# A two-layer decoder trunk in split fp32: a fourth Strassen block in the second MLP product, and the gate weights in the ring of activations

## The chip, the cores and the metric

One Trainium2 chip, one NeuronCore of it. The metric is the device time of one execution in microseconds; the figure for the kernel before is the median of three executions. Five engines appear in the profile: PE (TensorE, matrix products), DVE (VectorE), ACT (ScalarE), POOL (GpSimd) and SP (which only issues transfers here). Each engine works through its own list of instructions in a fixed order and waits on semaphores of the others.

## The reference, cut to what matters

Two layers, 256 tokens, width 2048. Layer 0 mixes by a gated convolution and differential attention, layer 1 by forgetting attention; after each comes a dense MLP with hidden width 8192:

```python
def _sqrelu_mlp(h, w1, w2):
    return jnp.square(jax.nn.relu(h @ w1)) @ w2
...
for l in range(DEPTH):
    ...                                   # mixer of the layer, added to x
    h = _rmsnorm(x, norm2_g[l])
    x = x + _sqrelu_mlp(h, mlp_w1[l], mlp_w2[l])
```

Layer 1's mixer also has a forget gate: 16 columns of `fox_w_in`, one per head, go through a log-sigmoid and a cumulative sum and become a bias on the logits.

## The kernel before

**Split products.** Every fp32 operand of a large product is split into a high part in the fp32r format (`wh`, a copy on ACT) and the rest (`wl`, a subtraction on DVE: `split_w`, L131). A product is then three matmuls: high by high, high by low, low by high (`products`, L619, the lines L620 to L622). A weight block of 4 x 512 columns is one DMA of 1 MB into a ring `wraw` of 3, and one `wh` and one `wl` out of rings of 3 (`wspl`).

**The MLP.** `mlp` (L685) takes the hidden width in four groups `g` of 2048. For each group `hidden` (L591) makes 16 column tiles of 128 of the squared ReLU, in eight pairs of tiles, by `gemm_t` (L531, matmuls L550 and L554). Then `gemm_pair` (L624) is called twice, for output columns 0 to 1023 (n = 0) and 1024 to 2047 (n = 2). I call one such call a *pair*: four groups, two calls, two layers make 16 pairs. A pair runs over eight blocks of weights, each 256 rows by 1024 columns, and the text `KINDS` (L560) says how each block is multiplied:

- `C`, classical: 2 row tiles x 4 output quarters x 3 matmuls = 24 matmuls of 512 columns, on one split of the raw block (DVE: one `wl` of 128x2048).
- `S`, Strassen's method in Winograd's form: 7 products x 3 = 21 matmuls. DVE first builds four sums of weight tiles `T` (L637, L639, L640), and then two splits follow, of three raw tiles (`wl` 128x1536) and of `T` (`wl` 128x2048, shown as `wl<-qk`).

All eight blocks add into eight PSUM banks, which is all there are: P2, Q3, Q4 and X out of the pool `acc` (4 banks), P1, Q5, P7 and P6 out of the pool `tp` (4 banks). P1, Q5, P7 and P6 get no more products after the last `S` block. So after the matmuls of the block that follows it (`if i == KINDS.rindex("S") + 1`, L664) they are combined into a tile `E`, and `E` is added into the residual `xr`: a copy on ACT (L666) and L667, L668, L669 and two L674 on DVE. I call these the *E chain*. The other four banks end with the eighth block; four L680 on DVE add them into `xr` (`final`). These are appended to `late` and emitted by the `flush` of the next product, which takes the four `acc` banks over from them: the next pair, or the next group's `gemm_t`, or layer 1's first projection (L165 to L167).

**What sets the order.** The lines are written in the order above, but a scheduler of the framework places the instructions of each engine when the program is built, by priority and its own estimates; the built order is then fixed. `order` listings in this document show that built order.

**Gate weights.** `gw` (the 16 gate columns) and `gws` (their split) have places of their own in the pool `const`; the load is in `setup` (L247), the split in `forget_gates` (L414, L418 and L419).

Of the kernel before, what the change touches and what calls it, by code (L numbers as in the profile page):

```python
# [8 lines left out]
F32 = mybir.dt.float32  # L9
F32R = mybir.dt.float32r  # L10
AF = mybir.ActivationFunctionType
ALU = mybir.AluOpType
# [14 lines left out]
def trunk_kernel(  # L27
# [199 lines left out]
    nlam = const.tile([P, 1], F32, name="nlam")  # L227
    bfb = const.tile([P, 16], F32, name="bfb")
    GP = 16 * 32 + 96
    gw = const.tile([P, KT, 16], F32, name="gw")  # L230
    gws = const.tile([P, GP], F32R, name="gws")

    def setup():
        rows = work.tile([P, 2 * P], F32, name="y")[:, :P]
# [9 lines left out]
        for i, v in enumerate((hyb_lq1, hyb_lk1, hyb_lq2, hyb_lk2)):  # L244
            nc.scalar.dma_start(lv[:, i, :], v.broadcast_to([P, 64]))
        nc.scalar.dma_start(bfb, fox_b_f.broadcast_to([P, 16]))
        nc.scalar.dma_start(gw, fox_w_in[0, :, 3 * D:3 * D + 16].rearrange("(k p) n -> p k n", p=P))  # L247


        nc.gpsimd.memset(mask, 0.0)  # L250
# [162 lines left out]

    def forget_gates(nm):  # L414

        wv = gws[:, :KT * 32].rearrange("p (k n) -> p k n", n=32)
        nc.scalar.copy(gws[:, KT * 32:], ones[:, :96])
        nc.scalar.copy(wv[:, :, 0:16], gw)  # L418
# [138 lines left out]

    KINDS = "SCSCSCCC"  # L560

    class PairS:

# [27 lines left out]
    def hidden(nm, w, c0):  # L591

        pairs, half = [], None
        for i, kind in enumerate(KINDS):
            acc = gemm_t(nm.acts, w, c0 + 2 * i * P)
            if kind == "S":
                p = PairS()
            elif half is not None:
                p, half = PairC(half), None
            elif "C" in KINDS[i + 1:]:  # L600
                t = actp.tile([P, 4, 2, 2 * P], F32R, name="act")
                p, half = PairC(t[:, :2]), t[:, 2:]
            else:
                p = PairC(qkv.tile([P, 2, 2, 2 * P], F32R, name="v"))
            pairs.append(p)

            def take(acc=acc, p=p):
                f = qkv.tile([P, 4, CW], F32, name="qk")[:, :2].rearrange("p a (f n) -> p (a f) n", n=P)
                for j in range(2):
                    fj = f[:, 2 * j:2 * j + 2].rearrange("p t n -> p (t n)")  # L610
                    nc.scalar.copy(fj, acc[j][:, 2 * P:])  # L611
                    nc.vector.tensor_tensor(fj, acc[j][:, :2 * P], fj, ALU.add)
                f4 = f[:, :4].rearrange("p t n -> p (t n)")
                nc.vector.scalar_tensor_tensor(f4, f4, 0.0, f4, ALU.max, ALU.mult)
                p.fill(f)
            late.append(take)
        return pairs
# [6 lines left out]
    def gemm_pair(pairs, w, r0, n, r2, done):  # L624

        B = {}
        live = set()
        for i, (kind, p) in enumerate(zip(KINDS, pairs)):
            raw = wraw.tile([P, 4, CW], F32, name="raw")
            nc.sync.dma_start(  # L630
                raw.rearrange("p (k h) n -> p k (h n)", k=2),
                w[r0 + 2 * i * P:r0 + 2 * (i + 1) * P, n * CW:(n + 2) * CW].rearrange("(k p) n -> p k n", p=P))

            more = KINDS[i + 1:]
            if kind == "S":
                T = qkv.tile([P, 4, CW], F32, name="qk")
                nc.vector.tensor_tensor(  # L637
                    T[:, 0:2], raw[:, 1:3], raw[:, 0:1].broadcast_to([P, 2, CW]), ALU.add)
                nc.vector.tensor_tensor(T[:, 2], T[:, 1], raw[:, 1], ALU.add)  # L639
                nc.vector.tensor_tensor(T[:, 3], T[:, 2], raw[:, 3], ALU.add)  # L640
                wa, wb = split_w(raw[:, 1:4]), split_w(T)
            else:
                wa = split_w(raw)
            if i == 0:
# [10 lines left out]
            if kind == "S":  # L655
                for bank, f, ws, j in (
                        ("P1", 0, wa, 0), ("P2", 2, wa, 2), ("Q3", 7, wa, 1),
                        ("Q5", 5, wb, 0), ("P7", 4, wb, 1), ("P6", 6, wb, 2), ("Q4", 3, wb, 3)):
                    mul(bank, p.part(f), ws, j, "S" not in more and bank in ("P1", "Q5", "P7", "P6"))
            else:  # L660
                for k in range(2):
                    for bank, t, h in (("P2", 0, 1), ("Q3", 0, 0), ("X", 1, 0), ("Q4", 1, 1)):
# [118 lines left out]
```

## Time and profile before

| | us |
|---|---|
| median of three executions | 2185.5 (2184.15 to 2185.83) |
| the profiled execution | 2182.76 |
| its span, first to last instruction | 2181.0 |
| PE busy | 2168.9 |
| DVE busy | 1546.9 |
| ACT busy | 1053.6 |
| granted TensorE clock, mean | 1.000 |

The profiled execution lies 2.7 us under the median. The end of a matmul is modelled in the profile and reaches past the start of the next, so how fast PE goes is read from the distance between starts, not from the duration of one.

### The profile page before, as it was taken

The numbers are of one execution on the slowest core, as the hardware profiler recorded it, in microseconds if no ns is written. First come the engines' busy times: TensorE is split into PE (matmuls) and PEld (weight loads), VectorE is DVE, ScalarE is ACT, GpSimd is POOL, SyncE is SP. The second block draws the span as 40 slices with busy tenths as digits, with TensorE's granted clock in tenths as the row PEclk, the third lists the DMA queues.
The fourth block names the chain that finished last, engine by engine and source line by source line (L and its number), as shares of the span: only waits on it lengthen the run. The fifth ranks groups of instructions, "written<-read, shape, count | busy, mean of one in ns | idle before, by whom it ended". The sixth has DMA issues, their size and how long they took to land.

```text
span 2181.0 us, 26007 instructions
## 1 busy us (share of the span) xinstructions
PE 2168.9 (99%) x10724; PEld 1822.0 (84%) x10724; DVE 1546.9 (71%) x1572; ACT 1053.6 (48%) x1099; POOL 18.8 (1%) x17
## 2 busy tenths in 40 slices
PE   8999999999999999999999999999999999999999
PEld 6887888888888888888888888888888888888887
DVE  5576555779768768867856565566787697687687
ACT  6465443545445444445554454445444444444453
POOL 0000000000000000000000000000000000000000
PEclk9999999999999999999999999999999999999999
DMA  7554555555765765665655555555556656656654
GB/s 258 174 173 155 178 189 193 176 172 197 221 186 173 227 191 179 214 189 183 209 168 190 188 182 173 180 174 180 166 205 217 191 174 217 191 187 210 186 193 152
DMA packets 245241, 412.08 MB, mean 189 GB/s; under 512 B 9367, under 2 KB 144770, under 8 KB 245122
## 3 DMA queue, kind: packets, MB, share of 16 engines
q1 hardware_dynamic: 237264, 405.84, 57.6%
q10 hardware_dynamic: 7858, 4.58, 0.7%
q8 instruction: 84, 1.38, 0.2%
q14 instruction: 35, 0.29, 0.0%
HBM read 408.28 MB, written 2.11 MB: 188 GB/s over the span
## 4 chain that ended last, share of the span: by engine, by line
PE 99%; DMA 0%; DVE 0%; ACT 0%; issue 0%; SPq 0%; ACTq 0%; DVEq 0%
PE acc L550 22%; PE acc L554 11%; PE acc L165 11%; PE acc L167 11%; PE acc L166 11%; PE acc L621 8%; PE acc L622 8%; PE acc L620 8%; PE tp L622 2%; PE tp L620 2%; PE tp L621 2%; PE tp L186 1%; PE tp L307 0%; PE tp L319 0%; PE tp L495 0%; DMA ob<-in_hyb_lk_dram 0%
## 5 line engine op out<-in xcount | busy, mean ns | idle before, releaser
L139 DVE TENSOR_TENSOR wl<-raw,wh 128x2048 fp32r<-128x2048 f32 (+2 forms) x388 | 853.6, 2202 | 485.9 <-ACT wh L138 485.3
L138 ACT CAST wh<-raw 128x2048 fp32r<-128x2048 f32 (+2 forms) x388 | 712.8, 1839 | 595.4 <-PE acc L167 219.2
L550 PE MATMUL acc<-act,wh 128*128 128x512 f32 x2048 | 559.6, 395 | 0.0
L165 PE MATMUL acc<-wh,act 128*128 128x512 f32 x1024 | 413.0, 404 | 1.7 <-ACT wh L138 1.7
L166 PE MATMUL acc<-wl,act 128*128 128x512 f32 x1024 | 401.3, 392 | 2.3 <-DVE wl L139 2.3
L167 PE MATMUL acc<-wh,act 128*128 128x512 f32 x1024 | 401.4, 392 | 0.0
L550 PEld LDWEIGHTS acc<-act,wh 128*128 128x128 f32 x2048 | 350.4, 189 | 47.9 <-DVE act L128 0.6
L554 PEld LDWEIGHTS acc<-act,wl 128*128 128x128 f32 x2048 | 314.2, 189 | 43.4
L554 PE MATMUL acc<-act,wl 128*128 128x256 f32 x2048 | 325.8, 281 | 0.0
L621 PE MATMUL acc<-wl,act 128*128 128x512 f32 x656 | 255.9, 390 | 0.0
L622 PE MATMUL acc<-wh,act 128*128 128x512 f32 x656 | 255.4, 389 | 0.0
L620 PE MATMUL acc<-wh,act 128*128 128x512 f32 x656 | 251.4, 389 | 0.0
L167 PEld LDWEIGHTS acc<-wh,act 128*128 128x128 f32 x1024 | 192.7, 188 | 41.9
L166 PEld LDWEIGHTS acc<-wl,act 128*128 128x128 f32 x1024 | 193.3, 189 | 40.9 <-DVE wl L139 3.5
L165 PEld LDWEIGHTS acc<-wh,act 128*128 128x128 f32 x1024 | 192.9, 189 | 40.3 <-ACT wh L138 2.1
L621 PEld LDWEIGHTS acc<-wl,act 128*128 128x128 f32 x656 | 123.1, 188 | 27.4 <-DVE wl L139 1.8
L620 PEld LDWEIGHTS acc<-wh,act 128*128 128x128 f32 x656 | 123.1, 188 | 25.7
L622 PEld LDWEIGHTS acc<-wh,act 128*128 128x128 f32 x656 | 123.1, 188 | 25.4
L138 ACT CAST wh<-qk 128x2048 fp32r<-128x2048 f32 x48 | 91.8, 1913 | 93.7 <-DVE qk L640 69.2
L139 DVE TENSOR_TENSOR wl<-qk,wh 128x2048 fp32r<-128x2048 f32 x48 | 110.0, 2291 | 27.5 <-ACT wh L138 27.5
L611 ACT COPY qk<-acc 128x256 f32<-128x256 f32 x128 | 47.1, 368 | 150.2 <-PE acc L554 150.2
L621 PE MATMUL tp<-wl,act 128*128 128x512 f32 x192 | 74.8, 389 | 0.0
(173 smaller groups left out, 1582.7 us busy)
## 6 DMA issues: line engine op xcount, KB each, us to landing
raw<-in_mlp_w_dram SPq DMA_DIRECT2D x256, 1024.0 KB, 5.6
raw<-in_fox_w_in_dram SPq DMA_DIRECT2D x48, 1024.0 KB, 5.1
raw<-in_hyb_w_in_dram SPq DMA_DIRECT2D x47, 1024.0 KB, 5.1
raw<-in_hyb_w_out_dram SPq DMA_DIRECT2D x16, 1024.0 KB, 5.1
raw<-in_fox_w_out_dram SPq DMA_DIRECT2D x16, 1024.0 KB, 5.0
ob<-fcd ACTq DMA_DIRECT2D x4, 512.0 KB, 4.6
xr<-in_x_dram SPq DMA_DIRECT2D x3, 512.0 KB, 6.8
raw<-in_hyb_w_in_dram SPq DMA_DIRECT2D x2, 512.0 KB, 5.4
```

Source lines behind the costliest of these rows:

```text
L138: nc.scalar.copy(wh[:, s], src[:, s])
L139: nc.vector.tensor_tensor(wl[:, s], src[:, s], wh[:, s].bitcast(F32), ALU.subtract)
L165: nc.tensor.matmul(acc[t], a.hi[:, k, ts], wh[:, k, :], start=st, stop=False)
L166: nc.tensor.matmul(acc[t], a.hi[:, k, ts], wl[:, k, :], start=False, stop=False)
L167: nc.tensor.matmul(acc[t], a.lo[:, k, ts], wh[:, k, :], start=False, stop=sp)
L186: nc.tensor.transpose(ps[:, t * P:(t + 1) * P], xr[n][:, t, j * P:(j + 1) * P], ident)
L550: nc.tensor.matmul(acc[f], wh[:, 4 * h + k, fs], a.both[:, k, :, :].rearrange("p s t -> p (s t)"), start=st, stop=False)
L554: nc.tensor.matmul(acc[f][:, 2 * P:], wl[:, 4 * h + k, fs], a.hi[:, k, :], start=False, stop=sp)
L611: nc.scalar.copy(fj, acc[j][:, 2 * P:])
L620: nc.tensor.matmul(acc, a[0], b[0], start=not started, stop=False)
L621: nc.tensor.matmul(acc, a[0], b[1], start=False, stop=False)
L622: nc.tensor.matmul(acc, a[1], b[0], start=False, stop=last)
```

## The change

- `KINDS` becomes `"SCSCSCSC"`: the seventh block of each pair is an `S` block instead of a `C` block. `KINDS.rindex("S") + 1` is thereby the eighth block instead of the sixth, which moves the E chain.
- `hidden` gives the seventh pair of tiles the Strassen form (`PairS`: three more small DVE sums, and a split of 128x1024 instead of 128x512). Sixth and eighth get a tile `v` each (before, the eighth alone).
- `gw` and `gws` give up their places in `const`: `gws` is a tile of the ring `act`, `gw` a work tile, and the load stands in `forget_gates`, with one more `yield` behind it.
- A kind `D` with a load through GpSimd is added to `load` and to the loop. No block has that kind, so its branches build no instruction. The scratch for dynamic DMA is 4096 instead of 1024.

```diff
-    gw = const.tile([P, KT, 16], F32, name="gw")
-    gws = const.tile([P, GP], F32R, name="gws")
...
-        nc.scalar.dma_start(gw, fox_w_in[0, :, 3 * D:3 * D + 16].rearrange("(k p) n -> p k n", p=P))
...
     def forget_gates(nm):
 
+        gt = actp.tile([P, 16 * P], F32R, name="act")
+        gws = gt[:, :GP]
+        gw = work.tile([P, 2 * P], F32, name="y").rearrange("p (k n) -> p k n", n=16)
+        nc.scalar.dma_start(gw, fox_w_in[0, :, 3 * D:3 * D + 16].rearrange("(k p) n -> p k n", p=P))
+        yield
...
-    KINDS = "SCSCSCCC"
+
+    KINDS = "SCSCSCSC"
...
-            elif "C" in KINDS[i + 1:]:
+            elif i < 3:
                 t = actp.tile([P, 4, 2, 2 * P], F32R, name="act")
                 p, half = PairC(t[:, :2]), t[:, 2:]
...
+        def load(i):
+            raw = wraw.tile([P, 4, CW], F32, name="raw")
+            src = w[r0 + 2 * i * P:r0 + 2 * (i + 1) * P, n * CW:(n + 2) * CW].rearrange("(k p) n -> p k n", p=P)
+            nc.sync.dma_start(raw.rearrange("p (k h) n -> p k (h n)", k=2), src)
+            if KINDS[i] != "D":
+                return raw, None
...
+        ahead = {}
         for i, (kind, p) in enumerate(zip(KINDS, pairs)):
-            raw = wraw.tile([P, 4, CW], F32, name="raw")
...
+            raw, wl = ahead.pop(i, None) or load(i)
+            if KINDS[i + 1:i + 2] == "D":
+                ahead[i + 1] = load(i + 1)
...
-    nc = _bacc.Bacc("TRN2", target_bir_lowering=False, num_devices=1, dynamic_dma_scratch_size=1024)
+    nc = _bacc.Bacc("TRN2", target_bir_lowering=False, num_devices=1, dynamic_dma_scratch_size=4096)
```

In the changed file the lines of the E chain are L693 (ACT) and L694, L695, L696, L701 (DVE), the final additions are L707, the sums of weights L654, L656, L657, the products L623 to L625.

**From the first pair of a group to the second, DVE.** The listing of before starts inside the E chain (L669, L674) and ends with the first split behind the final additions (L680). `wl` 128x1536 and `wl<-qk` are the splits of the second pair's first block, the last row that of its second block.

```order
L669 TENSOR_TENSOR qk<-tp,qk 128x2x512
L637 TENSOR_TENSOR qk<-raw 128x1024
L674 SCALAR_TENSOR_TENSOR xr<-qk,r_3689,xr 128x2x512 x2
L639 TENSOR_TENSOR qk<-qk,raw 128x512
L139 TENSOR_TENSOR wl<-raw,wh 128x1536
L640 TENSOR_TENSOR qk<-qk,raw 128x512
L637 TENSOR_TENSOR qk<-raw 128x1024
L639 TENSOR_TENSOR qk<-qk,raw 128x512
L680 SCALAR_TENSOR_TENSOR xr<-acc,r_3689,xr 128x512
L139 TENSOR_TENSOR wl<-qk,wh 128x2048
L680 SCALAR_TENSOR_TENSOR xr<-acc,r_3689,xr 128x512 x3
L139 TENSOR_TENSOR wl<-raw,wh 128x2048
```

The same place in the changed kernel, from the split of the eighth block on, which is now followed by the whole E chain:

```order
L139 TENSOR_TENSOR wl<-raw,wh 128x2048
L694 TENSOR_TENSOR qk<-tp,qk 128x512
L656 TENSOR_TENSOR qk<-qk,raw 128x512
L695 TENSOR_TENSOR qk<-tp,qk 128x512
L657 TENSOR_TENSOR qk<-qk,raw 128x512
L696 TENSOR_TENSOR qk<-tp,qk 128x2x512
L139 TENSOR_TENSOR wl<-raw,wh 128x1536
L701 SCALAR_TENSOR_TENSOR xr<-qk,r_3690,xr 128x2x512 x2
L139 TENSOR_TENSOR wl<-qk,wh 128x2048
L707 SCALAR_TENSOR_TENSOR xr<-acc,r_3690,xr 128x512 x4
L139 TENSOR_TENSOR wl<-raw,wh 128x2048
```

Between the split of the eighth block and the final additions there now stand the E chain and both splits of the next pair's first block. Before, the E chain stood two blocks of matmuls earlier: between it and the end of the pair PE had the seventh and the eighth block to do.

**From the second pair to the next group's `gemm_t`, DVE, before:** the two `wl` among the E chain are those of the seventh and the eighth block, the two behind it those of the next `gemm_t`.

```order
L139 TENSOR_TENSOR wl<-raw,wh 128x2048
L667 TENSOR_TENSOR qk<-tp,qk 128x512
L139 TENSOR_TENSOR wl<-raw,wh 128x2048
L668 TENSOR_TENSOR qk<-tp,qk 128x512
L139 TENSOR_TENSOR wl<-raw,wh 128x2048
L669 TENSOR_TENSOR qk<-tp,qk 128x2x512
L674 SCALAR_TENSOR_TENSOR xr<-qk,r_3689,xr 128x2x512 x2
L139 TENSOR_TENSOR wl<-raw,wh 128x2048 x2
L680 SCALAR_TENSOR_TENSOR xr<-acc,r_3689,xr 128x512 x4
```

In the changed kernel the two `wl` among the E chain are those of the next `gemm_t`:

```order
L139 TENSOR_TENSOR wl<-raw,wh 128x2048
L694 TENSOR_TENSOR qk<-tp,qk 128x512
L139 TENSOR_TENSOR wl<-raw,wh 128x2048
L695 TENSOR_TENSOR qk<-tp,qk 128x512
L139 TENSOR_TENSOR wl<-raw,wh 128x2048
L696 TENSOR_TENSOR qk<-tp,qk 128x2x512
L701 SCALAR_TENSOR_TENSOR xr<-qk,r_3690,xr 128x2x512 x2
L707 SCALAR_TENSOR_TENSOR xr<-acc,r_3690,xr 128x512 x4
```

The instructions and their order are the same as before up to the two updates of `xr`; what moved is the place of the row in the pair, by two blocks of matmuls.

**The first block of the second pair, PE, changed kernel** (buffer numbers kept: `tp_3998` is P1, `tp_3999`, `tp_4000`, `tp_4001` are Q5, P7, P6, `acc_3994` is P2; `wh_3982`, `wl_3983` are the split of the raw tiles, `wh_3986`, `wl_3987` that of the sums):

```order
L623 MATMUL tp_3998<-wh_3982,act_3069 128x512
L623 MATMUL tp_3999<-wh_3986,act_3069 128x512
L623 MATMUL tp_4000<-wh_3986,act_3069 128x512
L624 MATMUL tp_3998<-wl_3983,act_3069 128x512
L625 MATMUL tp_3998<-wh_3982,act_3069 128x512
L623 MATMUL tp_4001<-wh_3986,act_3069 128x512
L624 MATMUL tp_3999<-wl_3987,act_3069 128x512
L623 MATMUL acc_3994<-wh_3982,act_3069 128x512
L624 MATMUL acc_3994<-wl_3983,act_3069 128x512
```

Six matmuls stand ahead of the first that needs the low part of the sums, seven ahead of the first on a bank of the pool `acc`.

## Rows read from the trace of the kernel before

**Rows 1.** Page, busy time by engine: us (share of span) x instructions.

```profile
PE 2168.9 (99%) x10724; PEld 1822.0 (84%) x10724; DVE 1546.9 (71%) x1572; ACT 1053.6 (48%) x1099; POOL 18.8 (1%) x17
```

**Rows 2.** Page, the chain of work that ended last, by engine.

```profile
PE 99%; DMA 0%; DVE 0%; ACT 0%; issue 0%; SPq 0%; ACTq 0%; DVEq 0%
```

**Rows 3.** Timeline of PE: start us, us, engine line op; block starts of two pairs.

```profile
832.35 0.40 PE L620 MATMUL tp<-wh,act 128*128 128x512 f32 x1
...
852.79 0.39 PE L620 MATMUL tp<-wh,act 128*128 128x512 f32 x1
...
873.87 0.39 PE L620 MATMUL tp<-wh,act 128*128 128x512 f32 x1
...
894.29 0.39 PE L620 MATMUL tp<-wh,act 128*128 128x512 f32 x1
...
915.37 1.07 PE L550 MATMUL acc<-act,wh 128*128 128x512 f32 x4
```

**Rows 4.** Busy time in the two pairs: stretch, length; PE PEld DVE ACT POOL.

```profile
832.35:873.87 41.52, 41.52 (x185) 34.34 (x184) 36.70 (x30) 20.66 (x14) 0.00 (x0) 1.00 0.56 194
873.87:915.37 41.50, 41.50 (x184) 34.35 (x183) 35.74 (x26) 20.48 (x12) 0.00 (x0) 1.00 0.64 212
```

**Rows 5.** Timeline of DVE: the E chain and final additions of those pairs.

```profile
854.94 2.29 DVE L139 TENSOR_TENSOR wl<-raw,wh 128x2048 fp32r<-128x2048 f32 x1 [3.10 <-ACT wh L138]
857.15 0.69 DVE L667 TENSOR_TENSOR qk<-tp,qk 128x512 f32<-128x512 f32 x1
857.75 2.28 DVE L139 TENSOR_TENSOR wl<-raw,wh 128x2048 fp32r<-128x2048 f32 x1
...
862.75 1.22 DVE L669 TENSOR_TENSOR qk<-tp,qk 128x1024 f32<-128x1024 f32 x1
863.88 1.22 DVE L637 TENSOR_TENSOR qk<-raw 128x1024 f32<-128x1024 f32 x1
865.02 2.47 DVE L674 SCALAR_TENSOR_TENSOR xr<-qk,r,xr 128x1024 f32<-128x1024 f32 x2
867.41 0.68 DVE L639 TENSOR_TENSOR qk<-qk,raw 128x512 f32<-128x512 f32 x1
868.01 1.75 DVE L139 TENSOR_TENSOR wl<-raw,wh 128x1536 fp32r<-128x1536 f32 x1
869.68 0.69 DVE L640 TENSOR_TENSOR qk<-qk,raw 128x512 f32<-128x512 f32 x1
...
872.14 0.74 DVE L680 SCALAR_TENSOR_TENSOR xr<-acc,r,xr 128x512 f32<-128x512 f32 x1
872.80 2.28 DVE L139 TENSOR_TENSOR wl<-qk,wh 128x2048 fp32r<-128x2048 f32 x1
875.00 2.06 DVE L680 SCALAR_TENSOR_TENSOR xr<-acc,r,xr 128x512 f32<-128x512 f32 x3
876.98 2.28 DVE L139 TENSOR_TENSOR wl<-raw,wh 128x2048 fp32r<-128x2048 f32 x1
...
898.69 0.68 DVE L667 TENSOR_TENSOR qk<-tp,qk 128x512 f32<-128x512 f32 x1
...
907.95 2.29 DVE L139 TENSOR_TENSOR wl<-raw,wh 128x2048 fp32r<-128x2048 f32 x1
```

**Rows 6.** Timelines of DVE and PE: layer 1's first splits, end of the program.

```profile
1087.91 0.87 DVE L128 SCALAR_TENSOR_TENSOR act<-tp,g,act 128x256 fp32r<-128x256 f32 x2
...
2175.33 2.79 DVE L680 SCALAR_TENSOR_TENSOR xr<-acc,r,xr 128x512 f32<-128x512 f32 x4 [5.50 <-PE acc L622]
...
2176.94 0.39 PE L622 MATMUL acc<-wh,v 128*128 128x512 f32 x1
```

**Rows 7.** Instructions of the tile gw: its DMA from issue to landing, us.

```profile
DMA to landing us min/median/max: 6.0/6.0/6.0
```

**Rows 8.** Timeline of PE near the start of the program.

```profile
8.33 1.22 PE L165 MATMUL acc<-wh,act 128*128 128x512 f32 x2 [1.68 <-ACT wh L138]
...
10.18 0.63 PE L167 MATMUL acc<-wh,act 128*128 128x512 f32 x1
...
13.59 0.63 PE L167 MATMUL acc<-wh,act 128*128 128x512 f32 x1
```

More of the change, by code (lines that the diff above doesn't have):

```diff
@@ L627, in gemm_pair @@
         live = set()
+        def load(i):
[4 more added lines that the diff above has]
+                return raw, None
+            wl = wspl.tile([P, 4, CW], F32R, name="wl")
+            nc.scalar.activation(wl, raw, AF.Copy, scale=-1.0)
+            for k in range(2):
+                nc.gpsimd.dma_start(
+                    wl.rearrange("p (k h) n -> p k (h n)", k=2)[:, k], src[:, k], accum_op=ALU.add)
+            return raw, wl
+        ahead = {}
         for i, (kind, p) in enumerate(zip(KINDS, pairs)):
-            raw = wraw.tile([P, 4, CW], F32, name="raw")
-            nc.sync.dma_start(
-                raw.rearrange("p (k h) n -> p k (h n)", k=2),
-                w[r0 + 2 * i * P:r0 + 2 * (i + 1) * P, n * CW:(n + 2) * CW].rearrange("(k p) n -> p k n", p=P))
+            raw, wl = ahead.pop(i, None) or load(i)
+            if KINDS[i + 1:i + 2] == "D":
+                ahead[i + 1] = load(i + 1)
             more = KINDS[i + 1:]
@@ L641, in gemm_pair @@
                 wa, wb = split_w(raw[:, 1:4]), split_w(T)
+            elif kind == "D":
+                wa = wspl.tile([P, 4, CW], F32R, name="wh"), wl
+                nc.scalar.copy(wa[0], raw)
             else:
@@ L659, in gemm_pair @@
                     mul(bank, p.part(f), ws, j, "S" not in more and bank in ("P1", "Q5", "P7", "P6"))
+            elif kind == "D":
+                for q in (0, 2, 1):
+                    for k in range(2):
+                        for bank, t, h in (("P2", 0, 1), ("Q3", 0, 0), ("X", 1, 0), ("Q4", 1, 1)):
+                            nc.tensor.matmul(
+                                B[bank], p.part(k, t)[q // 2], wa[q % 2][:, 2 * k + h, :], start=bank not in live, stop=False)
+                            live.add(bank)
             else:
```

## The prediction

> **What bounds the kernel now.** I read the page's busy times first, then the chain that ended last, then the timelines of PE and DVE over the two pairs of one group. PE is busy for 2168.9 of 2181.0 us [rows 1], and 99% of the chain that ended last is PE [rows 2]: every matmul saved is time saved, if PE still finds its operands and banks ready. The pace is read from the starts. One pair runs from 832.35 to 873.87, the next to 915.37 [rows 3]: 41.52 and 41.50 us for 3 x 21 + 5 x 24 = 183 matmuls, which is 0.2268 us each, with no gap, also not where one pair gives its banks to the next. DVE is not far behind: 36.70 and 35.74 us of work in the same stretches [rows 4], some of the first being the hidden product's. So the question is not only whether DVE has the time, but whether it has it at the right place. Of a DVE instruction the distance to the next start is the price; its duration is some 0.07 longer and overlaps.
>
> **What the change removes.** One block per pair has 21 instead of 24 matmuls: 16 x 3 = 48, at 0.2268 us, is 10.9 us less for PE. This is the whole gain.
>
> **What it adds on DVE.** Prices from starts in [rows 5]: a sum of 1024 columns 1.14 (863.88 to 865.02), sums of 512 0.60 each (867.41 to 868.01), the split of 1536 1.67 (868.01 to 869.68), a split of 2048 2.20 (872.80 to 875.00). An S block costs 1.14 + 0.60 + 0.60 + 1.67 + 2.20 = 6.21, a C block 2.20. The E chain is 0.60 + 0.60 + 1.13 + 2.39 = 4.72, the four final additions 4 x 0.66 = 2.64. A pair before is 3 x 6.21 + 5 x 2.20 + 7.36 = 37.0 us against 41.5 on PE; after, 4 x 6.21 + 4 x 2.20 + 7.36 = 41.0 against 180 x 0.2268 = 40.8. By rate alone DVE just fails by 0.2 us. The larger form of the hidden tile (three small sums and twice the split, in all under 2 us a group) falls where DVE waits for ACT's copies, which wait for weight buffers: I take nothing for it, at worst 0.5 us a group (4 in all).
>
> **What it moves: the E chain.** This is the term that decides. Let t = 0 be PE's start on the last S block of a pair. Now that is the seventh block, so PE ends the pair at 45 x 0.2268 = 10.2 us; before it was the fifth, with three C blocks behind it. The E chain starts when P6 is complete and the split ahead of it is done: 857.15 against 852.79 and 898.69 against 894.29 [rows 3, 5], which is 4.4 us. The same split, waiting for the same ring of three, stands ahead of it now. What follows is fixed by the order shown.
>
> *From the first pair to the second, 8 places.* From 4.4: L694, L656, L695 and L657 at 0.60, L696 1.13, the split of 1536 1.67, two L701 2.39, the split of the sums 2.20. The first final addition starts at 14.2 and has ended (0.74) at 14.9. PE is done with the old pair at 10.2. Six matmuls need none of this; the seventh needs the split of the sums (14.3), the eighth a bank of the pool acc, all four of which are held until their L707 has read them (14.9). So PE stands from 11.6 to 14.3. It has 14 matmuls left of the block then and would end it at 18.1, but the second block's low part follows four L707 (to 16.8) and takes 2.29: 19.1, and only one matmul can go ahead of it. That block starts, in effect, at 18.9 instead of 15.0: 3.9 us lost. The third block's sums are late as well, since ACT's copy of them follows; PE has four high-part matmuls to do meanwhile, and I add 0.2. I take 4.1. The low bound is 3.1, the wait for the bank alone; the high one 4.8, if those four matmuls (0.9) cover nothing.
>
> *From the second pair to the next group, 6 places.* The seven DVE instructions from L694 to the second L701 are those from 898.69 to 907.95 of before, 9.26 us [rows 5]; the first L707 starts at 13.7, and its bank is free at 14.4. The next product's first matmul needs that bank; it could have started at 10.2. 4.2 us lost; 3.9 to 4.5, as the end of P6 alone (18 matmuls, 4.1) or a third of a microsecond of signalling decides. Before, the same instructions stood two blocks earlier and the row behind them waited for nothing that PE lacked.
>
> *From layer 0 to layer 1, one place.* As the last, with two L128 ahead of the final additions (0.87 [rows 6]): free at 15.3. PE does twelve small transposes meanwhile, about 1 us by my count: 4.0 lost, 3.0 to 5.1.
>
> *The end of the program.* E chain to 9.1, four L707, of which the last ends at 11.8. Before, the last ended at 2178.12, 0.95 us after PE's last matmul had made room for another (2176.94 + 0.23) [rows 6], in these terms 11.15. 0.7 us, 0 to 1.
>
> **What else moves.** The load of the gate weights goes from the start of the program to a later place on ACT's queue, behind the convolution's copies of layer 0; the copies that use it come in layer 1, hundreds of us later, and landing took 6.0 us [rows 7]. Nothing, and 6 us once if the cover were gone. The ring act has nine buffers: four of the norm, four outputs of attention, one for the gates, so none is missing. Kind D builds no instruction, and the scratch has no user. Zero for both.
>
> **The sum.** Lost: 8 x 4.1 + 6 x 4.2 + 4.0 + 0.7 = 62.7. Gained: 10.9. Net +51.8, against the profiled execution's 2182.8: 2234.6. The median of the runs lies 2.7 above that execution: **2237**. With all low bounds (25 + 23 + 3 - 10.9 = +40) 2226, with all high ones, the hidden tile's 4 among them, 2250.
>
> [...]
>
> **Rival: DVE works ahead, and it is faster.** The place is the same. If the final additions reached the first bank within 10.2 + 7 x 0.227 = 11.8 us of the last S block's start, instead of 14.9, PE would not stop there, and DVE's 0.2 us too much per pair would be all: 2182.8 - 10.9 + 16 x 0.2 + 2.7 = 2177.8. For it: total DVE work fits, and before, the same hand-over cost nothing. Against: the E chain cannot start before P6 is complete, and 9.8 us of listed instructions stand between it and the first final addition. The order would have to differ from the one shown.
>
> **Rival: the change is neutral.** If the stalls were a fifth as long, 12 us, gain and loss would cancel: 2186. No row gives such a price.
>
> **How the numbers follow.** About 0.2% (4.4 us) is what a measurement of this kernel can tell from no change. Forecast, 2222 to 2250 around 2237: 0.72. The clock, above 2250: 0.14. Slower with shorter stalls, 2190 to 2222: 0.05. Faster: 0.06. Within 0.2%: 0.03. From 2222 upward to the clock's own 2264 the range holds the forecast and over half of that rival: 0.72 + 0.08. I set 2222 to 2264. Slower in all: 0.72 + 0.14 + 0.05 = 0.91.
>
> **What would show it right or wrong.** Right: in the profile after, the PE waits list L623 or L552 waiting for DVE's L707 and for wl of the sums, about 4 us at each of some 15 places, nothing inside the pairs; a pair's own matmuls 0.227 apart and 180 of them; the first L707 14 us after PE's start on the seventh block. PE's busy share falls to about 97%, and the slices around hand-overs show an 8. [...] The fast rival: no such waits, and PE's chain 10.9 us shorter. I am wrong if P6's completion no longer starts the E chain, or if PE finds other work at the hand-over than the order shows.

## The result and the profile after

The changed kernel is slower: 2267.0 us (median of 5 runs, 2262.3 to 2268.2) against 2185.5; the ratio is 1.0374, 95% interval 1.0362 to 1.0385. The direction was forecast, the size was not: 81.5 us are lost where the sum said 51.8, and 2267 lies 3 us above the range. The profiled execution took 2266.4 us, its span is 2263.6.

From the page: busy time by engine and the chain that ended last, which answer to [rows 1, 2]; then, from the list of cores, span and mean granted clock:

```profile
PE 2195.1 (97%) x10676; PEld 1830.6 (81%) x10676; DVE 1620.1 (72%) x1660; ACT 1080.5 (48%) x1115; POOL 18.0 (1%) x17
...
PE 78%; DVE 14%; DMA 4%; issue 2%; ACT 2%; SPq 0%; DVEq 0%; ACTq 0%
```

```profile
core 0: 2263.6 us, clock 0.986
```

PE has 48 matmuls fewer and is busy for 26 us more. So matmuls have become slower, and the granted clock agrees: 0.986 on the mean of the span, where it was 1.000 before. The chain now runs through VectorE for 14%.

PE's waits in the whole run (total in us, times, the longest):

```profile
PE acc L552 <- DVE xr L707: 25.0, 6, 4.2
PE tp L624 <- DVE wl L139: 21.0, 9, 2.6
PE acc L624 <- DVE wl L139: 4.1, 9, 0.8
...
PE tp L186 <- DVE act L128: 2.4, 1, 2.4
```

The first row is the 6 places behind a second pair, the second row holds the 8 between the pairs of a group, the last is the layer boundary. The third was not forecast: waits inside pairs.

The timeline of VectorE at one first pair and at the second pair behind it, which answers to [rows 5] (start, length, instruction, idle time before it). PE had started the last S block at 885.83 and at 932.55:

```profile
886.75 1.23 DVE L654 TENSOR_TENSOR qk<-raw 128x1024 f32<-128x1024 f32 x1 [2.34 <-DMA raw<-in_mlp_w_dram]
...
890.19 0.69 DVE L694 TENSOR_TENSOR qk<-tp,qk 128x512 f32<-128x512 f32 x1
...
895.39 2.48 DVE L701 SCALAR_TENSOR_TENSOR xr<-qk,r,xr 128x1024 f32<-128x1024 f32 x2
897.78 2.29 DVE L139 TENSOR_TENSOR wl<-qk,wh 128x2048 fp32r<-128x2048 f32 x1
899.98 2.72 DVE L707 SCALAR_TENSOR_TENSOR xr<-acc,r,xr 128x512 f32<-128x512 f32 x4
902.62 2.28 DVE L139 TENSOR_TENSOR wl<-raw,wh 128x2048 fp32r<-128x2048 f32 x1
...
936.95 0.68 DVE L694 TENSOR_TENSOR qk<-tp,qk 128x512 f32<-128x512 f32 x1
...
946.19 2.72 DVE L707 SCALAR_TENSOR_TENSOR xr<-acc,r,xr 128x512 f32<-128x512 f32 x4
```

Counted from the S block, the E chain starts at 4.36 and 4.40 (forecast 4.4), the first final addition at 14.15 and 13.64 (14.2 and 13.7), the split behind the additions at 16.8 (16.8). The ledger of VectorE's instructions was right to a tenth.

The timeline of PE at the same two hand-overs:

```profile
896.71 0.39 PE L624 MATMUL tp<-wl,act 128*128 128x512 f32 x1
896.94 0.39 PE L625 MATMUL tp<-wh,act 128*128 128x512 f32 x1
897.17 0.39 PE L623 MATMUL tp<-wh,act 128*128 128x512 f32 x1
900.12 0.80 PE L624 MATMUL tp<-wl,act 128*128 128x512 f32 x1 [2.57 <-DVE wl L139]
900.78 0.80 PE L623 MATMUL acc<-wh,act 128*128 128x512 f32 x1
901.38 0.63 PE L624 MATMUL acc<-wl,act 128*128 128x512 f32 x1
901.80 0.63 PE L625 MATMUL acc<-wh,act 128*128 128x512 f32 x1
...
905.64 0.63 PE L623 MATMUL acc<-wh,act 128*128 128x512 f32 x1
906.07 0.53 PE L624 MATMUL acc<-wl,act 128*128 128x512 f32 x1
906.44 0.39 PE L625 MATMUL acc<-wh,act 128*128 128x512 f32 x1
906.67 0.40 PE L623 MATMUL acc<-wh,act 128*128 128x512 f32 x1
...
942.52 0.39 PE L625 MATMUL acc<-wh,v 128*128 128x512 f32 x1
947.08 1.84 PE L552 MATMUL acc<-act,wh 128*128 128x512 f32 x4 [4.17 <-DVE xr L707]
```

Ahead of the first wait the matmuls start 0.23 us apart, behind it 0.42 to 0.43 for some 5 us (901.38 to 901.80), as at the program's start (0.43, eight distances from 10.18 to 13.59 [rows 8], where the profile gives a granted clock of 1.00), and then 0.23 again (906.44 to 906.67). The granted clock of the slow stretch, the third number from the end of this row, is half:

```profile
901.40:906.00 4.60, 4.60 (x12) 3.61 (x11) 4.60 (x5) 1.47 (x1) 0.00 (x0) 0.50 0.04 6
```

So these matmuls ran at a granted clock of 0.50. Behind the second wait four matmuls take 1.84 us. The same follows 14 of the 15 waits, with a stretch at a granted clock of 0.50 at each of them; behind the first wait inside a group of layer 1 (2.57 us, ending at 1664.85) the granted clock is 1.00 and the distances stay at 0.23 to 0.24. The forecast gives the clock a chance and a time of its own, 2264; here its slow matmuls come on top of the forecast's waits and not in place of them.

VectorE's own wait for raw weights, in the kernel before and in the changed one:

```profile
DVE qk L637 <- DMA raw<-in_mlp_w_dram: 4.7, 13, 0.7
```

```profile
DVE qk L654 <- DMA raw<-in_mlp_w_dram: 41.4, 24, 2.6
```

An S block's raw weights stay in their buffer until VectorE has read them several times, and the ring has three. SP's queue, which loads the next block, waits for that. Its own list of waits, before and after:

```profile
SPq L630 <- DVE wl L139: 458.5, 104, 8.9
```

```profile
SPq L634 <- DVE wl L139: 510.3, 96, 9.3
```

The queue stood for the ring before too, so these rows alone do not show that the ring is too short; the run with four buffers below tests it. The loads themselves are not slower: 5.5 us from issue to landing, 5.6 before. With four S blocks VectorE reaches the sums before the weights have landed; one such wait (2.34) stands in the rows above, just ahead of the E chain.

### The profile page after: what moved, and what is told of

It reads as the page before. It is cut to its first block, busy times and chain, and to the rows that moved or that the text cites. A ratio compares the mean times of both kernels' runs of the same rounds, so it can differ in the third digit from the quotient of the medians.

```text
span 2263.6 us, 26026 instructions
## 1 busy us (share of the span) xinstructions
PE 2195.1 (97%) x10676; PEld 1830.6 (81%) x10676; DVE 1620.1 (72%) x1660; ACT 1080.5 (48%) x1115; POOL 18.0 (1%) x17
## 4 chain that ended last, share of the span: by engine, by line
PE 78%; DVE 14%; DMA 4%; issue 2%; ACT 2%; SPq 0%; DVEq 0%; ACTq 0%
PE acc L552 21%; PE acc L556 11%; PE acc L165 10%; PE acc L167 10%; PE acc L166 10%; DVE wl L139 7%; DMA raw<-in_mlp_w_dram 3%; PE acc L624 3%; PE acc L625 3%; PE acc L623 3%; ACT wh L138 2%; DVE xr L701 1%; PE tp L624 1%; DVE qk L654 1%; PE tp L625 1%
## 5 line engine op out<-in xcount | busy, mean ns | idle before, releaser
L552 PE MATMUL acc<-act,wh 128*128 128x512 f32 x2048 | 569.1, 400 | 25.0 <-DVE xr L707 25.0
L165 PE MATMUL acc<-wh,act 128*128 128x512 f32 x1024 | 414.2, 405 | 3.1 <-ACT wh L138 2.8
L166 PE MATMUL acc<-wl,act 128*128 128x512 f32 x1024 | 402.2, 393 | 2.2 <-DVE wl L139 2.2
L167 PE MATMUL acc<-wh,act 128*128 128x512 f32 x1024 | 401.5, 393 | 0.1
L167 PEld LDWEIGHTS acc<-wh,act 128*128 128x128 f32 x1024 | 193.3, 189 | 43.5 <-DVE act L128 1.2
L165 PEld LDWEIGHTS acc<-wh,act 128*128 128x128 f32 x1024 | 193.3, 189 | 42.1 <-ACT wh L138 3.2
L166 PEld LDWEIGHTS acc<-wl,act 128*128 128x128 f32 x1024 | 193.6, 189 | 40.9 <-DVE wl L139 3.3
L138 ACT CAST wh<-qk 128x2048 fp32r<-128x2048 f32 x64 | 122.4, 1912 | 184.5 <-DVE qk L657 122.9
L139 DVE TENSOR_TENSOR wl<-qk,wh 128x2048 fp32r<-128x2048 f32 x64 | 146.5, 2289 | 54.9 <-ACT wh L138 54.8
L623 PE MATMUL acc<-wh,act 128*128 128x512 f32 x448 | 178.7, 399 | 0.8 <-DVE xr L707 0.8
L624 PE MATMUL acc<-wl,act 128*128 128x512 f32 x448 | 178.4, 398 | 0.5 <-DVE wl L139 0.5
L625 PE MATMUL acc<-wh,act 128*128 128x512 f32 x448 | 177.7, 397 | 0.0
L624 PE MATMUL tp<-wl,act 128*128 128x512 f32 x256 | 103.0, 402 | 21.1 <-DVE wl L139 21.0
L654 DVE TENSOR_TENSOR qk<-raw 128x1024 f32<-128x1024 f32 x64 | 78.1, 1221 | 41.5 <-DMA raw<-in_mlp_w_dram 41.4
L624 PE MATMUL acc<-wl,v 128*128 128x512 f32 x256 | 101.0, 394 | 3.7 <-DVE wl L139 3.7
L623 PEld LDWEIGHTS acc<-wh,act 128*128 128x128 f32 x448 | 85.7, 191 | 21.4 <-DVE xr L707 3.5
```

What stands on the lines that cost most here:

```text
L138: nc.scalar.copy(wh[:, s], src[:, s])
L139: nc.vector.tensor_tensor(wl[:, s], src[:, s], wh[:, s].bitcast(F32), ALU.subtract)
L165: nc.tensor.matmul(acc[t], a.hi[:, k, ts], wh[:, k, :], start=st, stop=False)
L166: nc.tensor.matmul(acc[t], a.hi[:, k, ts], wl[:, k, :], start=False, stop=False)
L167: nc.tensor.matmul(acc[t], a.lo[:, k, ts], wh[:, k, :], start=False, stop=sp)
L552: nc.tensor.matmul(acc[f], wh[:, 4 * h + k, fs], a.both[:, k, :, :].rearrange("p s t -> p (s t)"), start=st, stop=False)
```

## The experiments

My theory after the result: three things add up, the waits as forecast, a low clock after them, and raw weights that land late. The rival: VectorE's rate alone, 41.0 us of work a pair against 40.8 on PE. Each kernel was timed beside the kernel before (2184.6 to 2185.5 in the four sets). Line numbers of the kernels shift by a few; the operations are the same.

**The gate weights alone.**

```diff
-    KINDS = "SCSCSCSC"
+    KINDS = "SCSCSCCC"
-            elif i < 3:
+            elif "C" in KINDS[i + 1:]:
```

> The changed kernel with the seventh block classical again (row of kinds SCSCSCCC, rule for the hidden tiles as before); the gate weights stay in the ring of activations. It tells whether the gate part of the change has any share in the 81 us. Theory 'waits and clock' (15 hand-overs at which PE waits for VectorE, and a lower clock after each): no share, 2185.5, within 2 us of the kernel before, granted clock 1.00. Rival 'ring' (the late load of the gate weights or the fuller ring of activations delays something): up to 6 us more, 2188 to 2192, with a PE wait of some us where the forget gates are worked out in layer 1.

2184.9 us, ratio 0.9999 (0.9990 to 1.0009). The gate weights, the fuller ring and the scratch have no share. The whole loss comes from the seventh block being an S block, with the form of the hidden tile that goes with it.

**PE kept busy in the waits.** Eleven matmuls that nobody reads ahead of a second pair's first block, eighteen (fill) ahead of the product behind a second pair.

```diff
+                if n == 2:
+                    t0 = p.t.rearrange("p a s n -> p (a s n)")
+                    for _ in range(11):
+                        nc.tensor.matmul(B["P6"], t0[:, :P], t0[:, :CW], start=True, stop=True)
...
+                if fill:
+                    d = tpp.tile([P, CW], F32, name="tp")
+                    for _ in range(fill):
+                        nc.tensor.matmul(d, acts[0].hi[:, 0, :P],
+                            acts[0].both[:, 0].rearrange("p s t -> p (s t)"), start=True, stop=True)
```

> The changed kernel, with matmuls that nobody reads placed in PE's waits: 11 of 512 columns ahead of the second pair of a group (8 places, 2.5 us against a wait of 2.6), 18 ahead of the product that follows a second pair (6 places, 4.1 us against 4.2). VectorE has the same work in the same order, so every wait for it ends when it ended before. Theory 'waits and clock': PE no longer stands still, the clock stays up, matmuls after the fillers are 0.227 us apart instead of 0.427, and the time falls by nearly 30 us: 2239, 2234 to 2246, which is the forecast without the clock rival. Rival 'VectorE late' (the 30 us not forecast are VectorE being late in the blocks behind the hand-over too, and the slow matmuls wait for its results): no change, 2264 to 2272, or a little slower where the fillers run past the end of a wait.

2249.8 us: 17.2 less, with a granted clock of 0.997. PE's timeline, at the same two places:

```profile
892.25 2.66 PE L678 MATMUL tp<-act 128*128 128x512 f32 x11
...
897.37 0.39 PE L628 MATMUL acc<-wh,act 128*128 128x512 f32 x1
897.60 0.39 PE L629 MATMUL acc<-wl,act 128*128 128x512 f32 x1
...
937.47 4.24 PE L548 MATMUL tp<-act 128*128 128x512 f32 x18
942.25 1.16 PE L557 MATMUL acc<-act,wh 128*128 128x512 f32 x4 [0.54 <-DVE xr L716]
```

Extra matmuls made the kernel faster: behind them the distances are 0.23, and the four matmuls of L557 take 1.16 instead of 1.84. The clock is shown as a cause. But 2249.8 is above the 2234 to 2246 expected, so it is not the only one. The 17.2 need not be the clock's alone either: the expectation had VectorE's order unchanged, but in the built order a first sum of weights and a split have changed places in all eight second pairs. The pair of runs with four buffers below does not have this flaw.

**Four buffers for raw weights.** Room for the fourth comes from single buffers for two small tiles of attention and a smaller scratch.

```diff
-    wraw = ctx.enter_context(tc.tile_pool(name="wraw", bufs=3))
+    wraw = ctx.enter_context(tc.tile_pool(name="wraw", bufs=4))
```

> The changed kernel with four buffers for raw weights instead of three (room made by single buffers for two small tiles of attention and a smaller scratch, which no line of the MLP uses). In the changed kernel VectorE's first sum of weights waits 41.4 us in all for the landing of raw weights, which the forecast did not have. Theory 'late loads' (these waits make VectorE late and are the other part of what was not forecast): PE's waits of 0.5 to 1 us inside the pairs go and those at the hand-over get shorter, 2267 - 8 to 20: 2247 to 2259. Rival 'place alone' (the E chain's start, not the loads, sets the hand-over): VectorE's waits for raw weights go, PE's waits stay, 2262 to 2268; what attention gains or loses by its single buffers shows outside the MLP.

2254.3 us, 12.6 less. VectorE's waits for raw weights are gone from the list, PE's waits inside the pairs nearly so, the hand-overs stay. (With the fourth buffer the scheduler also placed some of VectorE's instructions in another order; the 12.6 are buffer and order together.)

```profile
PE acc L552 <- DVE xr L707: 24.8, 6, 4.1
PE tp L624 <- DVE wl L139: 20.5, 8, 2.6
...
PE acc L624 <- DVE wl L139: 0.5, 1, 0.5
```

**Both, and the control.** The same two edits together; and the fourth buffer in the kernel with three S blocks.

> The changed kernel with both: matmuls that nobody reads in PE's waits (11 and 18, as before) and four buffers for raw weights. Theory 'two causes' (a low clock after the waits, and raw weights that land late): 2267.0 - 17.2 - 12.7 = 2237, 2232 to 2242, which is what the sum of the forecast gave for the waits alone; granted clock above 0.995. Rival 'same time twice' (slow matmuls hide part of VectorE's lateness, and the two savings overlap): 2244 to 2252.

> The run with the gate weights in the ring and three Strassen blocks a pair, with four buffers for raw weights, two single buffers in attention and the smaller scratch. Theory 'two causes': PE waits for nothing in the MLP of this kernel, so a fourth buffer gives nothing: 2185, 2182 to 2188. Rival 'general gain': the fourth buffer helps elsewhere too (start of the program, products of attention), 2172 to 2181; what the single buffers cost in attention would show as 2188 to 2195.

Both: 2242.2 us, clock 0.999. That is just past the upper end of what "two causes" allowed (2242), below "same time twice" (from 2244): 5 us of the two savings overlap. The control: 2181.3, ratio 0.9983 (0.9974 to 0.9993), between its two expectations: the fourth buffer gives a little without the change as well. The difference of these two, 60.9 us, is what the change costs with the clock up and the weights there in time.

With four buffers the idle matmuls leave VectorE's built order exactly as it was, so the 12.2 us between 2254.3 and 2242.2 are theirs. Where they come from shows in the length of one second pair and of the hidden product behind it, without idle matmuls and with them (columns: window, its length, PE, PEld, DVE, ACT, POOL, granted clock, DMA):

```profile
892.29:938.02 45.73, 43.16 (x181) 34.44 (x179) 40.41 (x31) 21.85 (x13) 0.00 (x0) 0.96 0.61 191
938.02:1034.63 96.61, 92.47 (x514) 80.60 (x513) 65.40 (x68) 40.59 (x39) 0.00 (x0) 0.96 0.60 182
```

```profile
888.67:934.39 45.72, 44.56 (x193) 35.51 (x191) 40.41 (x31) 21.85 (x13) 0.00 (x0) 1.00 0.61 191
934.39:1028.56 94.17, 94.12 (x532) 81.77 (x530) 65.38 (x68) 40.62 (x39) 0.00 (x0) 1.00 0.62 187
```

The second pair takes as long with slow matmuls as with fast ones, at all eight places: what it needs from VectorE and ScalarE comes no earlier, and the slow matmuls cost nothing there. Behind the second pairs PE sets the pace, and the six hidden products, which took between 95.7 and 97.0 us, take 94.2: 12.5 us in all.

What PE still waits for in the kernel with both:

```profile
PE acc L628 <- ACT wh L138: 4.8, 8, 0.6
PE tp L628 <- ACT wh L138: 3.8, 8, 0.5
```

That is the third block of a second pair: its sums are late, ScalarE's copy of them too, and PE waits 1.1 us a place, for which I had 0.2. With four buffers and slow matmuls only one wait for ScalarE, of 0.5 us, stands in the pairs: the time spent in slow matmuls covered the others.

**The E chain left out.**

```diff
-                E = qkv.tile([P, 4, CW], F32, name="qk")
-                nc.scalar.copy(E[:, 3], B["P1"])
...
-                    nc.vector.scalar_tensor_tensor(x2, e, r2[:, t:t + 1], x2, ALU.mult, ALU.add)
```

> The changed kernel without the E chain: the four sums and the two additions that bring P1, Q5, P7 and P6 into the result are left out (4.72 us on VectorE and one copy on ACT for each pair), everything else stays, so part of the result is missing. Theory 'waits and clock': the first final addition starts at 9.5 instead of 14.2 after the last S block's start, the bank is free before PE wants it, and nearly the whole loss goes: 2174 to 2182, clock 1.00. Rival 'VectorE late' (rate of sums and splits, and loads of raw weights that come late): less than half of it goes, 2215 to 2245, since sums, splits and loads stay.

2190.9 us, clock 1.00: 76 of 81.5 us go, but it stays 9 above the range. No hand-over is among PE's waits; those inside the pairs are, and with them VectorE's wait for raw weights:

```profile
PE acc L624 <- DVE wl L139: 7.4, 15, 0.9
```

```profile
DVE qk L654 <- DMA raw<-in_mlp_w_dram: 31.2, 17, 2.5
```

So the E chain's work at the hand-over sets the 4 us waits, and late weights cost separately.

**The same work in another order.** The two additions of the E chain go into final(), behind the four L707. (In this kernel a part of the last result is sent out ahead of these additions.)

```diff
-                    nc.vector.scalar_tensor_tensor(x2, e, r2[:, t:t + 1], x2, ALU.mult, ALU.add)
-                done(0)
+                hold.append(E)
```

> The changed kernel with the two additions of the E chain (L701, 2.39 us) moved behind the four final additions of the pair: the same work on VectorE, in another order. Theory 'place' (what stands ahead of the first final addition sets PE's wait): the wait for the bank falls from 4.3 to about 1.5 us at the 6 places behind a second pair, the wait of 2.6 at the 8 places inside a group goes but comes back as smaller ones, since the split of the second block still comes behind the additions; with shorter waits the clock stays up. 2267 - 6 x 2.9 - 17 = 2233, 2224 to 2246, granted clock above 0.995. Rival 'amount' (VectorE's total of work per pair sets the pace, wherever it stands): no gain beyond 5 us, 2260 to 2268.

2227.4 us: 39.6 less, with no instruction less. Place, not amount. The waits behind second pairs are gone from the list, where 1.5 us each were expected to stay; the other kind has moved to the second block's low part, as the expectation said, but it has hardly become smaller:

```profile
PE acc L624 <- DVE wl L139: 20.6, 16, 2.4
```

The clock is 0.992, not above 0.995: with these waits, of 2.4 us at the longest, it still falls.

**The S block moved forward.**

```diff
-    KINDS = "SCSCSCSC"
+    KINDS = "SCSSCSCC"
-            elif i < 3:
+            elif KINDS[:i].count("C") < 2:
```

> The changed kernel with the kinds in the order SCSSCSCC: the same four blocks by Strassen's method and 48 matmuls fewer, but two classical blocks behind the last of them, so that the E chain and the final additions have 21 + 48 matmuls of cover as VectorE had it before. Theory 'waits and clock' (the place of the E chain makes the waits): they go, and with them the low clock; 2185.5 - 10.9 = 2174.6, with up to 0.2 us a pair for VectorE's rate 2178; range 2172 to 2184. Rival 'VectorE late' (41.0 us of work a pair against 40.8 on PE, and too short rings): waits of about 1 us inside the pairs, 2190 to 2215.

2208.1 us. Here my theory lost: the big waits and the low clock (0.999) are gone, yet it is 23 us slower than before instead of 11 faster. Busy time in a first pair and the second pair behind it (columns as above), and rows of the two engines' timelines:

```profile
840.75:881.75 41.00, 41.00 (x183) 33.73 (x181) 37.40 (x31) 22.02 (x15) 0.00 (x0) 1.00 0.52 180
881.75:925.74 43.99, 42.79 (x181) 33.14 (x179) 40.87 (x31) 21.86 (x14) 0.00 (x0) 1.00 0.66 214
```

```profile
907.73 0.68 DVE L657 TENSOR_TENSOR qk<-qk,raw 128x512 f32<-128x512 f32 x1
910.46 2.29 DVE L139 TENSOR_TENSOR wl<-qk,wh 128x2048 fp32r<-128x2048 f32 x1 [2.05 <-ACT wh L138]
```

```profile
927.21 1.16 PE L552 MATMUL acc<-act,wh 128*128 128x512 f32 x4 [1.31 <-DVE xr L707]
```

The first pair takes 41.0 us and loses 0.2, the second takes 44.0 and loses 3. VectorE's load differs: in the second pair, where the first pair's final additions come in, it has 40.9 us of work in 44.0, against 37.4 in 41.0. Of the 3.1 us left, 2.05 are one stop between the sums and their split, for ScalarE's copy in between. So 41.0 against 40.8 was no near tie but a loss of 3 us in every second pair. That such stops are what VectorE lacks is my reading; no run takes them away, and the first pair, with less work, has the same stop without that loss. The last row shows something else: behind a wait of 1.31 us the four matmuls take 1.16, against 1.84 behind the 4.17 in the changed kernel.

**Moved forward, other variants.** SCSSCSCC with the two additions, now add(), called in final() where hold is true (not in a layer's last group); and SCSCSSCC with the same and four buffers.

```diff
+                if not hold:
+                    add()
...
+            if hold:
+                add()
```

> Kinds in the order SCSSCSCC, and the two additions of the E chain behind the four final additions, except in the last group of a layer, where they stay. Theory 'place': the wait of 1.4 us for the bank behind a second pair goes (6 places, 8 us), and the four smaller waits at the start of a second pair get shorter: 2208 - 8 - up to 8: 2192 to 2201. Rival 'amount': VectorE's work in a pair is the same, and the waits come back at the next block, 2203 to 2209.

> Kinds in the order SCSCSSCC with the E chain's additions behind the final additions (but for the last group of a layer) and four buffers for raw weights. Theory 'amount' (VectorE's 41 us a pair leave it no reserve, wherever the blocks stand): the two neighbouring Strassen blocks at the end of the pair make PE wait there instead, 2194 to 2210. Rival 'place': without the neighbours near the hand-over of SCSSCSCC the sums keep ahead, 2174 to 2186.

2204.6 us: the wait of 1.3 us behind second pairs goes, but in its place PE waits 10.9 us (8 times, longest 1.7) for the second block's low part; "amount" was nearer here. 2193.3 us for the other, just under the range of "amount", with PE waiting for ScalarE's copies at every second pair. Both clocks are 1.00, with waits of up to 1.7 us. Of the orders tried this one loses least, but it is the only one of them with four buffers: against the control with four buffers (2181.3) it is 12 us slower, and it gives nothing of the 10.9 us.

**Work taken off VectorE.** Three ideas in five kernels: E scaled on ScalarE and added on GpSimd, in the changed kernel and with SCSSCSCC; the first sum of weights on GpSimd, with SCSSCSCC; the last block's low part made by an adding DMA (kind D: SCSSCSCD and SCSCSCSD; the flag that ends a bank's sum, which kind D lacked, is set there too).

```diff
-                    nc.vector.scalar_tensor_tensor(x2, e, r2[:, t:t + 1], x2, ALU.mult, ALU.add)
+                    nc.scalar.activation(e, e, AF.Copy, scale=r2[:, t:t + 1])
+                    nc.gpsimd.tensor_tensor(x2, e, x2, ALU.add)
...
-                nc.vector.tensor_tensor(
+                nc.gpsimd.tensor_tensor(
                     T[:, 0:2], raw[:, 1:3], raw[:, 0:1].broadcast_to([P, 2, CW]), ALU.add)
...
-    KINDS = "SCSCSCSC"
+    KINDS = "SCSCSCSD"
```

> The changed kernel with the two additions of the E chain taken off VectorE: ScalarE scales E in place, GpSimd adds it to xr (by the 2.07 us of GpSimd's product of 512 columns, some 4 us for each 1024). VectorE has 2.39 us less in each of 16 pairs, the order is otherwise the same. Theory 'amount' (VectorE's work at the hand-over): each wait falls by 2.4 us, 16 x 2.4 = 38, and what is left is too short to lower the clock, 17 more: 2267 - 55 = 2212, 2202 to 2224. Rival 'shared' (GpSimd beside VectorE slows VectorE, or the tile of E is held too long): VectorE's instructions beside GpSimd's are longer than the 2.29 us of a split, and less than half is gained, 2240 to 2262.

> Kinds in the order SCSSCSCC, as in the run with that order, and the E chain's additions on ScalarE and GpSimd, as in the run with those. VectorE then has 41.0 - 2.4 = 38.6 us a pair against 40.8 on PE. Theory 'amount' (in the run with SCSSCSCC a pair took 43.1 us because VectorE had no reserve, 2208 in all): the pairs come down to 40.8 to 41.3, 2174 to 2184, under the kernel before. Rival 'chain' (the sums, ScalarE's copy of them and their split follow one another with VectorE idle for 2 us an S block, for lack of buffers): the pairs stay above 42, 2195 to 2208. Rival 'shared': VectorE slows beside GpSimd, 2190 to 2215, seen in longer splits.

> Kinds in the order SCSSCSCC, E chain as before, and the first sum of weights of each S block (1024 columns, 1.14 us on VectorE) on GpSimd, some 4 us there: VectorE has 4 x 1.14 = 4.6 us less in a pair, but each S block's sums start a chain that is 3 us longer. Theory 'amount': the pairs come down from 43.1 to about 41, 2172 to 2186. Rival 'chain' (latency from the landing of raw weights to the split of their sums, in a ring of three): slower than with VectorE alone, 2208 to 2260, with PE waiting for ScalarE's copy of the sums.

> Kinds in the order SCSSCSCD: as the run with SCSSCSCC, but the low part of the last block's weights is made without VectorE: ScalarE writes the negated, rounded weights, and a DMA issued by GpSimd adds the raw weights to them; 2.2 us less for VectorE in each pair, 1 MB more to read. Theory 'amount' (VectorE has no reserve in the run with SCSSCSCC, pairs of 43.1 us): the pairs come down to 41 to 42, 2174 to 2192. Rival 'landing' (the adding DMA lands later than a split would): PE waits for wl of the last block, 2208 to 2240.

> The changed kernel's order of kinds with the last classical block's low part made by an adding DMA (SCSCSCSD): no split of 2.2 us stands ahead of the E chain. Theory 'place and clock': every wait at a hand-over falls by 2.2 us, what is left is 0.5 to 2.1 and does not lower the clock: 2267 - 15 x 2.2 - 17 = 2217, 2205 to 2230, granted clock above 0.995. Rival 'landing': the E chain also waits for P6, and PE waits for the adding DMA instead, 2245 to 2275.

All slower than the same kernel without the edit (2267.0 for the first and the last, 2208.1 for the others), and above every range expected: 2308.7, 2247.0, 2272.0, 2242.3 and 2293.4 us. For the first the list of VectorE's waits and GpSimd's group tell why:

```profile
DVE xr L708 <- POOL xr L702: 63.0, 24, 4.6
```

```profile
L702 POOL TENSOR_TENSOR xr<-qk,xr 128x1024 f32<-128x1024 f32 x32 | 95.0, 2987 | 1922.8 <-ACT qk L701 1922.8
```

The final additions write the same part of xr, so they wait for GpSimd, whose addition of 1024 columns takes 2.99 us against 1.2 on VectorE. I had counted VectorE's instructions and not who waits for the result; the splits beside GpSimd kept their 2.29, so "shared" was wrong in its mechanism too. With the sum on GpSimd, PE waits 55.0 us in 36 places for the low part of the sums: the rival "chain", but 12 us above its range. For kind D I can only say where it waits, not why in full: in the last kernel PE stands up to 10.5 us for the final additions, and VectorE waits for PE at a split, probably for a buffer that PE still reads, since D's tile takes one of the three; no run shows that this is the cause:

```profile
DVE wl L139 <- PE acc L624: 30.2, 8, 3.8
```

## Why the prediction was wrong

The step that failed is the place of the clock in the forecast ("How the numbers follow"). The clock was made a rival, with a chance of 0.14 and a time of its own, 2264, that would *replace* the forecast. That PE goes at the full pace between the waits protects nothing: in the changed kernel it does for 36 us between the two waits shown (906.44 to 942.52, granted clock 1.00), and behind 14 of the 15 waits the matmuls were 0.43 us apart. The term belonged in the sum, where it was put at nothing. Measured, it is 12.2 us with the weights in time.

The rival's price was wrong in another way. The 27 us between 2237 and 2264 were an estimate: nine matmuls behind each of 15 waits, 0.20 us slower each, the difference between the distances of 0.43 in [rows 8] and 0.227 in a pair; no row of the kernel before shows them behind a wait of this kind. They were a fair count of slow matmuls: added up from the distances behind the 15 waits, the time over the full pace is 27 to 29 us, in the changed kernel and with four buffers. But of the 27 with four buffers 12 lie behind the eight waits inside a group, where the second pair ends no later for them. Only the 13 behind the six second pairs and the 2 at the layer boundary lengthen the kernel. So the price of a low clock is the slow matmuls at the places where PE itself sets the pace behind the wait.

Two more terms failed with it. Late raw weights were put at nothing, and cost 8.4 us. The waits at full clock were 71.8 us and not 62.7, mostly by the third block of a second pair.

The account, in us. Its last column is made of differences of five medians and adds up by construction; what tests the parts are the rows above. The kernel before differed by up to 0.9 us between the sets, so single tenths mean little.

| part | forecast | measured |
|---|---|---|
| matmuls saved | -10.9 | -10.9, by count and pace |
| waits at full clock, weights in time (both edits against the control, and the 10.9) | +62.7 | 60.9 + 10.9 = +71.8 |
| low clock (2254.3 - 2242.2; without the fourth buffer 2267.0 - 2249.8) | 0, as rival 27 | +12.2 (17.2) |
| late raw weights (2267.0 - 2254.3, less the control's 4.3) | 0 | +8.4 |
| sum | +51.8 | +81.5 |

Point by point, with starts from the kernel with both edits and from its control:

- *The matmuls saved.* Right: with both edits a first pair takes 40.82 us from start to start (847.85 to 888.67), 180 x 0.2268.
- *The E chain and the order of VectorE.* Right to 0.1 us, as the rows after show.
- *First to second pair, 4.1.* With both edits 86.54 for two pairs (847.85 to 934.39), 4.9 more than 2 x 40.82 and just above the high bound of 4.8. The wait was nearly right (2.8, forecast 2.7). The second block lost 0.3, where the forecast had 1.2: PE found more high-part matmuls to do meanwhile than the one that the sum allowed. The third block lost 1.7, where it had 0.2: 1.1 waiting for ScalarE and the rest in smaller gaps. The 4.1 was near in part by luck, two errors that work against each other. 8 x 0.8 = 6.4.
- *Second pair to next group, 4.2.* 4.4 (94.17 for the hidden phase against 89.79), within the bounds. The high bound's third of a microsecond of signalling is 0.15 in the changed kernel (an addition of 0.74 from 946.19, PE at 947.08). It is the wait alone: in the kernel without the E chain, which has no such wait, the hidden phase takes 89.79 as before, so the larger form of the hidden tile costs nothing, as assumed.
- *Layer boundary, 4.0.* 4.5, within the bounds: from the start of layer 0's last group to layer 1's first pair 578.09 (1028.56 to 1606.65) against 570.02 (1005.01 to 1575.03), of which 3.5 are the two pairs.
- *The end of the program, 0.7.* 1.3, a little above the high bound of 1: 91.62 from the start of the last group (2148.75 to 2240.37) against 86.83 (2093.44 to 2180.27), less the same 3.5.
- *"Nothing inside the pairs".* Wrong. VectorE's rate was compared with PE's in sums of work; that the ring of three would make it wait for loads was not looked at. With the fourth buffer the waits for loads are gone.
- *Gate weights, ring, kind D.* Zero, as said.

The rival "DVE works ahead" did not come true: the first final addition started where the order put it. In the orders tried later the work fits by its sum and PE still waits; that ScalarE's copy between two of VectorE's steps is the reason is argued from the rows, not shown.

## What to carry to other kernels

Where a change makes the busy engine stand for some microseconds at many places (here 2.4 to 4.2 us at 15, with matmuls 0.43 us apart instead of 0.23 behind 14 of them), add the slow matmuls behind each wait to the sum, as a term, but only where that engine sets the pace behind the wait; and before trusting a wait's price, fill it with work nobody needs and see what comes back. Where a second engine comes within a few per cent of the first, its total says little: write down its chain through the other engines and the rings that feed it. Moving the order of the same instructions (39.6 us gained) was worth more than moving work to an idle engine (42 us lost), because the idle engine's result was waited for.

## What the runs showed of the hardware

In the changed kernel the granted clock fell to 0.50 at 14 of 15 waits of 2.4 to 4.2 us, and matmuls of 512 columns were 0.43 us apart behind them for a few microseconds; in the pairs of the kernel before, at 1.00, they are 0.23 apart. Not every such wait does it: behind one of 2.57 us, ending at 1664.85, the granted clock was 1.00 and the distances 0.23 to 0.24. With SCSSCSCC, behind a wait of 1.31 us, four matmuls took 1.16 us, and the mean clock was 0.999 with six waits of up to 1.4 us there; with the additions moved as well, the longest wait was 1.7 us and the mean clock 1.00. Eleven and eighteen idle matmuls a hand-over, 196 in all, took 17 us off the changed kernel and 12 off the one with four buffers, where VectorE's order stayed the same. GpSimd added 1024 fp32 columns in 2.99 us, against 2.07 for its product of 512 columns in the changed kernel.
